# The first microseconds of a two-layer hybrid block: input in eight pieces in turn with weights, four dummy matmuls, and a yield between two groups of 32-row transposes

## The chip, the cores and the metric

The kernel runs on one core of a Trainium2 chip. The metric is the device time of one execution in microseconds (us); 2110.56 us is the median of three runs of the kernel before (2109.86 to 2110.83). Engines are named as in the profile: PE is the matrix engine (PEld its weight loads), DVE the vector engine, ACT the scalar engine, POOL the general one, SP the engine that issues most DMAs. "Granted clock" is the share of its full clock that PE was given, as the profile records it.

## The reference

The input x is 256 tokens by 2048. Layer 0 normalizes x, projects it, runs an S5 state-space mixer on one half and a gated recurrence (HGRN2) on the other, projects back and adds; then comes an MLP. Layer 1 does the same with sliding-window attention. Cut to what matters here:

```python
def rms_norm(x, gain):
    y = x * lax.rsqrt(jnp.mean(x * x, axis=-1, keepdims=True) + EPS)
    return y * gain

def reference(x, ...):
    h = x
    for layer in range(2):
        if layer == 0:
            y = s5_hgrn2_layer(rms_norm(h, even_norm[0]), even_w_in[0], ...)  # first product: xn @ w_in
        else:
            y = attention_layer(rms_norm(h, odd_norm[0]), ...)
        h = h + y
        h = h + squared_relu_mlp(rms_norm(h, mlp_norm[layer]), mlp_w_up[layer], mlp_w_down[layer])
    return h

# inside s5_mixer: B is scaled by a factor that is computed at run time
bbr = zr[..., None] * br - zi[..., None] * bi
bbi = zr[..., None] * bi + zi[..., None] * br
```

## The kernel before, in words

**Products.** Every weight matrix is cut into units of 512 KB, 704 in all, listed in the order of use in `units`. A unit is fetched into a tile `raw` (`emit_dma`, L86, four buffers), rounded to the 32-bit matmul type by ACT (`whi`, L93), and DVE subtracts to get the rest (`wlo`, L94). The activations are split in the same way into `XT.hi` and `XT.lo`. A product is three matmuls into one PSUM accumulator `acc`: whi times hi, whi times lo, wlo times hi (`mm`, L124, called by `wblock`, `ublock` and `xblock`). `advance` fetches up to six units ahead and splits up to three ahead, as far as buffers allow. In the first two blocks one unit holds two slices k of 128 rows and serves 24 matmuls of 256 columns.

**Start.** SP fetches x in four pieces of 512 columns (`load_x`, L244), with four weight units between them. ACT fetches the constants `cf` (with the identity) and the gain `even_norm`. PE runs eight dummy matmuls on a zeroed tile (`WARM`, L253), then turns the gain into columns (`vturn`, L270). Then `make_xT` transposes x: four transposes of 128 by 128 (L293) fill one PSUM tile with two slices k, ACT scales and rounds each into `XT0.hi` (L296), DVE makes `XT0.lo` (L297). With all four pieces listed ahead, the block loop begins: `wblock(XT0, K16)` for the first 512 columns of `even_w_in`.

**Side work.** Small work is written as generators in the list `side`. After each unit `pump(SIDE)` lets the first generator go on until it has yielded 1.5 us by its own estimates. `norm0` computes the row norms, `s5_prep` prepares the S5 matrices: in it 32 transposes (L436) turn the two halves of `Bn`, 16 each, from 32 partitions by 128 into 128 by 32. `s5_main` and `hgrn` follow. Their results are needed at fixed points, where `drain` runs them out. After the ten column blocks of `even_w_in`, the S5 result is split into `yg` (ACT L783, DVE L784), and the gate product `w_glu` starts.

**Order.** The code order is not the final one: a scheduler with a timeline model of its own merges the streams and decides each engine's order, so that a small edit moves instructions far behind it. What counts is each engine's final list, shown below for the places that matter.

Of the kernel before, what the change touches and what calls it, by code (L numbers as in the profile page):

```python
# [8 lines left out]
F32 = mybir.dt.float32  # L9
# [5 lines left out]
ALU = mybir.AluOpType  # L15
AX = mybir.AxisListType

P = 128
# [6 lines left out]
SIDE = 1.5  # L25
LOOK = 3
WARM = 8
LOOK_DMA = 6

NCF = 128 + 256 + 32 + 2  # L30
# [26 lines left out]
def hybrid_kernel(ctx: ExitStack, tc: tile.TileContext, x, even_norm, even_w_in, s5_lambda_re, s5_lambda_im,  # L57
                  s5_log_dt, s5_b_re, s5_b_im, s5_c_re, s5_c_im, s5_d, s5_w_glu, s5_b_glu, hgrn_lower_bound,
                  hgrn_o_norm, even_w_out, odd_norm, odd_w_qkv, q_norm, k_norm, att_sinks, odd_w_out,
                  mlp_norm, mlp_w_up, mlp_w_down, cfd, cmd, out, stop=None):  # L60
    nc = tc.nc
    V, S, G, PE = nc.vector, nc.scalar, nc.gpsimd, nc.tensor
# [10 lines left out]
    units = []  # L73
# [6 lines left out]
    raws, splits = {}, {}  # L80
    ptr = {"dma": 0, "split": 0, "use": 0}

    def emit_dma(i):
        W, kt, n0, nk = units[i]
        raw = wp.tile([P, nk, 1024 // nk], F32, tag="raw", name="raw", bufs=4)
        nc.sync.dma_start(out=raw, in_=W[kt * P:(kt + nk) * P, n0:n0 + 1024 // nk].rearrange("(k p) n -> p k n", p=P))  # L86
        raws[i] = raw

    def emit_split(i):
        raw, nk = raws.pop(i), units[i][3]  # L90
        hi = wp.tile([P, nk, 1024 // nk], F32R, tag="whi", name="whi")
        lo = wp.tile([P, nk, 1024 // nk], F32R, tag="wlo", name="wlo")
        S.copy(out=hi, in_=raw)  # L93
        V.tensor_tensor(out=lo, in0=raw, in1=hi.bitcast(F32), op=ALU.subtract)  # L94
        splits[i] = (hi, lo)

    def advance():
        i = ptr["use"]
        while ptr["dma"] < min(len(units), i + LOOK_DMA + 1) or ptr["split"] < min(len(units), i + LOOK + 1):
            if ptr["dma"] < min(len(units), i + LOOK_DMA + 1) and ptr["dma"] < ptr["split"] + 4:  # L100
                emit_dma(ptr["dma"])
                ptr["dma"] += 1
            else:
                emit_split(ptr["split"])
                ptr["split"] += 1
        ptr["use"] += 1
        return splits.pop(i)
# [67 lines left out]
    def pm(shape, dtype=F32):  # L175
        return psM.tile(shape, dtype, tag="m", name="m")

    def t4(shape, dtype=F32):
        return sp.tile(shape, dtype, tag="t4", name="t4")
# [60 lines left out]
    xt = cp.tile([P, 2, D], F32, tag="h", name="xt", bufs=1)  # L240
    xv = x[0].rearrange("(t p) n -> p t n", p=P)

    def load_x(q):
        nc.sync.dma_start(out=xt[:, :, q * 512:(q + 1) * 512], in_=xv[:, :, q * 512:(q + 1) * 512])  # L244

    cf = cp.tile([P, 130], F32, name="cf")
    load_x(0)
# [1 line left out]
    warm = t4([P, 512], BF16)  # L249
    V.memset(warm, 0.0)  # L250
    wps = pm([P, 512])
    for _ in range(WARM):
        PE.matmul(wps, warm[:, 0:P], warm, start=True, stop=True, skip_group_check=True)  # L253
    ident = cf[:, 0:128]
# [18 lines left out]
    def vc(name, i=0):  # L273
        k, c = vcol[name]
        return vec[k][:, c + i:c + i + 1]
# [1 line left out]
    vrow(0, "g0", even_norm.rearrange("o (k p) -> (o k) p", p=P), 16)  # L277
    cmt = cp.tile([P, 8, P], U8, tag="cm", name="cmt", bufs=1)

    for q, n in ((1, 1), (2, 2), (3, 0)):  # L280
        for _ in range(n):
            emit_dma(ptr["dma"])
            ptr["dma"] += 1
        load_x(q)
    vturn(0)

    def make_xT(src, XT, gain, kt0, nk):

        for a in range(kt0, kt0 + nk, 2):
            ps = pm([P, 2, T])  # L290
            for b in range(2):
                for t in range(2):
                    PE.transpose(ps[:, b, t * P:(t + 1) * P], src[:, t, (a + b) * P:(a + b + 1) * P], ident)  # L293
            for b in range(2):
                g = vc(gain, a + b)
                ihi = S.activation(out=XT.hi[:, a + b, :], in_=ps[:, b, :], func=AF.Copy, scale=g)  # L296
                ilo = V.scalar_tensor_tensor(out=XT.lo[:, a + b, :], in0=ps[:, b, :], scalar=g,  # L297
                                             in1=XT.hi[:, a + b, :].bitcast(F32), op0=ALU.mult, op1=ALU.subtract)
        return ihi, ilo

    XT0 = new_pair("x")
    for q in range(4):
        lastx = make_xT(xt, XT0, "g0", 4 * q, 4)


    rsx = cp.tile([P, 2], F32, name="rsx")
# [35 lines left out]
    def s5_prep():  # L342

        W = P
# [88 lines left out]
        for ri in range(2):  # L433
            bb = pm([P, 16, 32])
            for c in range(16):
                PE.transpose(bb[:, c, :], Bn[:, ri, :].rearrange("m (x c) -> m x c", c=16)[:, :, c],  # L436
                             ident[0:32, 0:32])
            bps.append(bb)

        def bc(v):  # L440
            return v.unsqueeze(1).to_broadcast([P, 16, 32])
# [19 lines left out]
        for ri in range(2):  # L461
# [3 lines left out]
            for h in range(2):  # L465
                ps = pm([P, 4, P])
                for f in range(4):
                    PE.transpose(ps[:, f, :], Cm[:, h * 4 + f].rearrange("p g w -> p (g w)"), ident)  # L468
                S.activation(out=CX[:, 0, ri, h * 16:h * 16 + 16, :].rearrange("p m c -> p (m c)"),
                             in_=ps.rearrange("p f w -> p (f w)"), func=AF.Copy, scale=-1.0 if ri else 1.0)  # L470
# [16 lines left out]
        for ri in range(2):  # L487
# [5 lines left out]
            for a in range(0, 16, 4):  # L493
                ps = pm([P, 4, P])
# [250 lines left out]
    for i in range(10):  # L745
# [3 lines left out]
        if i < 2:  # L749
            drain(n00)  # L750
            while "UY" not in st:
                pump(0.1)
            V.tensor_tensor(out=st["UY"][:, 4 * i:4 * i + 4, :], in0=acc,
                            in1=rsb.unsqueeze(1).to_broadcast([P, 4, T]), op=ALU.mult)
# [10 lines left out]
        for a in range(2):  # L765
            if j < 2:
                d2 = dst[:, a].rearrange("p (m t) -> p m t", m=2)
                V.tensor_tensor(out=d2, in0=acc[:, 2 * a:2 * a + 2, :],
                                in1=rsb.unsqueeze(1).to_broadcast([P, 2, T]), op=ALU.mult)
# [18 lines left out]
    for n in range(2):  # L788
# [4 lines left out]
        for a in range(2):  # L793
# [4 lines left out]
                            op=ALU.subtract)  # L798
# [86 lines left out]
    n0 = residual(yT, out0_passes, (lambda: Norm("g1")) if stop != "mix0" else Out, hwait)  # L885
# [145 lines left out]
    for t in range(2):  # L1031
        ps = pm([P, 4, P])
        for g in range(4):
# [4 lines left out]
                               in1=ka[0:64, :, ts_].bitcast(F32), op0=ALU.mult, op1=ALU.subtract)  # L1038
# [45 lines left out]
```

## Time and profile before

| what | value |
|---|---|
| three runs, median | 2110.56 us (2109.86 to 2110.83) |
| the profiled execution's own time | 2110.3 us |
| its span, first to last instruction | 2108.4 us |
| outside the span | 1.9 us |
| PE busy | 2096.6 us (99%) |
| DVE busy, ACT busy | 1333.9 us (63%), 1031.2 us (49%) |
| HBM read | 375.18 MB |

The profile is of one execution. Matmuls are pipelined, so that one lasts longer than the distance to the next; what a matmul costs is that distance. A line with a releaser ("<-") tells what ended an engine's idle time. The chain of waits is followed back from the last instruction. A window row gives for a stretch of time the busy time of an engine, the number of its instructions, the granted clock, the DMA engines' busy share and their rate.

### The profile page before, as it was taken

The page shows a single profiled execution, that of the slowest core. Times are in us where ns is not written, and L with a number is a line of the kernel's source. Part 1 is how long each engine was busy: PE and PEld are TensorE (multiplying, and loading weights), DVE is VectorE, ACT ScalarE, POOL GpSimd, SP SyncE. Part 2 cuts the span into 40 slices and gives each one's busy share as a digit, 9 for nine tenths or more (in the row PEclk, how much of TensorE's full clock was granted, in tenths as well). Part 3 has the DMA queues.
Part 4 walks back from the last instruction along what each step waited for, and adds up shares of the span by engine and source line. Part 5 has one row for each costly group of instructions (what it writes and reads, how often), then busy time and mean ns, then how long its engine had stood idle before and what let it go on. Part 6 is the DMA issues. An engine that isn't in the chain of part 4 may idle for free.

```text
span 2108.4 us, 29603 instructions
## 1 busy us (share of the span) xinstructions
PE 2096.6 (99%) x11628; PEld 1790.4 (85%) x11628; DVE 1333.9 (63%) x1859; ACT 1031.2 (49%) x1379; POOL 36.2 (2%) x36
## 2 busy tenths in 40 slices
PE   9999999999999999999999999999999999999999
PEld 8988888888888888888888888788888888888887
DVE  6799968765655565555555588765665565555544
ACT  5876554454443444344345477564443444344332
POOL 1000000000000000000000110000000000000000
PEclk8999999999999999999999999999999999999999
DMA  7455554566656666666656644456656666665664
GB/s 243 131 151 159 182 160 150 161 182 189 184 188 193 190 186 192 195 183 189 196 189 183 190 150 130 140 172 189 186 185 195 192 183 192 196 185 187 197 201 149
DMA packets 262859, 379.20 MB, mean 180 GB/s; under 512 B 14040, under 2 KB 145536, under 8 KB 262400
## 3 DMA queue, kind: packets, MB, share of 16 engines
q1 hardware_dynamic: 261296, 374.04, 57.6%
q0 software_dynamic: 672, 2.15, 0.3%
q8 instruction: 91, 1.49, 0.3%
q10 hardware_dynamic: 752, 1.12, 0.1%
q14 instruction: 48, 0.39, 0.1%
HBM read 375.18 MB, written 2.10 MB: 179 GB/s over the span
## 4 chain that ended last, share of the span: by engine, by line
PE 99%; DVE 0%; DMA 0%; ACT 0%; issue 0%; SPq 0%; DVEq 0%; ACTq 0%
PE acc L124 93%; PE m L124 4%; PE m L293 1%; PE m L977 1%; DMA xt<-in_x_dram 0%; PE m L436 0%; PE m L1011 0%; ACT whi L93 0%; PE m L496 0%; PE m L468 0%; DVE t L637 0%; PE m L718 0%; DVE t L613 0%; DVE clo L613 0%; DVE wlo L94 0%; DVE h L836 0%
## 5 line engine op out<-in xcount | busy, mean ns | idle before, releaser
L94 DVE TENSOR_TENSOR wlo<-raw,whi 128x1024 fp32r<-128x1024 f32 x704 | 861.9, 1225 | 687.2 <-ACT whi L93 686.7
L93 ACT CAST whi<-raw 128x1024 fp32r<-128x1024 f32 x704 | 738.7, 1050 | 973.7 <-PE acc L124 848.0
L124 PE MATMUL acc<-x,whi 128*128 128x512 f32 (+1 forms) x2944 | 893.9, 365 | 1.0 <-ACT x L783 1.0
L124 PE MATMUL acc<-x,wlo 128*128 128x256 f32 x2496 | 705.1, 283 | 0.0
L124 PEld LDWEIGHTS acc<-x,whi 128*128 128x128 f32 x2944 | 528.4, 190 | 97.6 <-ACT x L783 1.1
L124 PE MATMUL acc<-whi,chi 128*128 128x512 f32 x1280 | 500.1, 391 | 0.2 <-DVE h L836 0.2
L124 PE MATMUL acc<-whi,clo 128*128 128x512 f32 x1280 | 499.0, 390 | 0.0
L124 PE MATMUL acc<-wlo,chi 128*128 128x512 f32 x1280 | 498.9, 390 | 0.0
L124 PEld LDWEIGHTS acc<-x,wlo 128*128 128x128 f32 x2496 | 474.7, 190 | 1.5 <-issue 0.6
L124 PEld LDWEIGHTS acc<-whi,chi 128*128 128x128 f32 x1280 | 240.4, 188 | 50.5 <-issue 1.2
L124 PEld LDWEIGHTS acc<-whi,clo 128*128 128x128 f32 x1280 | 240.4, 188 | 49.5
L124 PEld LDWEIGHTS acc<-wlo,chi 128*128 128x128 f32 x1280 | 240.4, 188 | 48.9
L124 PE MATMUL acc<-whi,x 128*128 128x512 f32 x576 | 181.6, 393 | 0.0
L124 PEld LDWEIGHTS acc<-whi,x 128*128 128x128 f32 x576 | 107.5, 188 | 22.3 <-issue 1.0
L124 PE MATMUL acc<-wlo,x 128*128 128x512 f32 x288 | 113.3, 393 | 0.0
L124 PEld LDWEIGHTS acc<-wlo,x 128*128 128x128 f32 x288 | 54.1, 188 | 10.7
L866 DVE SCALAR_TENSOR_TENSOR h<-acc,rs2g,h 128x512 f32<-128x512 f32 x64 | 45.1, 747 | 21.3 <-PE acc L124 21.3
L852 DVE SCALAR_TENSOR_TENSOR t<-t 128x512 f32<-128x512 f32 x64 | 44.3, 692 | 2.2
L855 DVE TENSOR_TENSOR clo<-t,chi 128x512 fp32r<-128x512 f32 x64 | 43.8, 685 | 0.0
L851 DVE TENSOR_TENSOR t<-acc,t 128x512 f32<-128x512 f32 x64 | 43.8, 684 | 0.0
L854 ACT CAST chi<-t 128x512 fp32r<-128x512 f32 x64 | 39.3, 614 | 0.0
L850 ACT COPY t<-acc 128x512 f32<-128x512 f32 x64 | 37.0, 578 | 0.0
(204 smaller groups left out, 936.3 us busy)
## 6 DMA issues: line engine op xcount, KB each, us to landing
raw<-in_mlp_w_up_dram SPq DMA_DIRECT2D x256, 512.0 KB, 3.7
raw<-in_mlp_w_down_dram SPq DMA_DIRECT2D x256, 512.0 KB, 3.7
raw<-in_even_w_in_dram SPq DMA_DIRECT2D x80, 512.0 KB, 4.1
raw<-in_odd_w_qkv_dram SPq DMA_DIRECT2D x40, 512.0 KB, 3.6
raw<-in_even_w_out_dram SPq DMA_DIRECT2D x32, 512.0 KB, 3.7
raw<-in_odd_w_out_dram SPq DMA_DIRECT2D x32, 512.0 KB, 3.8
raw<-in_s_w_glu_dram SPq DMA_DIRECT2D x8, 512.0 KB, 3.8
xt<-in_x_dram SPq DMA_DIRECT2D x4, 512.0 KB, 8.4
```

The lines of the kernel that those rows point to most:

```text
L93: S.copy(out=hi, in_=raw)
L94: V.tensor_tensor(out=lo, in0=raw, in1=hi.bitcast(F32), op=ALU.subtract)
L124: PE.matmul(o, a, b, start=start, stop=stop, skip_group_check=True, **kw)
L293: PE.transpose(ps[:, b, t * P:(t + 1) * P], src[:, t, (a + b) * P:(a + b + 1) * P], ident)
L850: S.copy(out=r, in_=acc[:, :, 1])
L851: V.tensor_tensor(out=r, in0=acc[:, :, 0], in1=r, op=ALU.add)
L852: V.scalar_tensor_tensor(out=r, in0=r, scalar=0.0, in1=r, op0=ALU.max, op1=ALU.mult)
L854: S.copy(out=ch[c].hi[:, ks, :], in_=r)
L855: V.tensor_tensor(out=ch[c].lo[:, ks, :], in0=r, in1=ch[c].hi[:, ks, :].bitcast(F32), op=ALU.subtract)
L866: V.scalar_tensor_tensor(out=h[:, t, cs], in0=acc[:, t], scalar=norm.rs2[:, t:t + 1], in1=h[:, t, cs], op0=ALU.mult, op1=ALU.add)
L977: PE.transpose(ps[:, r, a, :], pr[:, 2 * a + r, k * P:(k + 1) * P], ident)
```

## The change

Five things are done. x is fetched in eight pieces of 256 columns (256 KB) instead of four of 512, with one weight unit between two pieces; pieces 5 to 7 are listed behind the fetch of weight units 4 to 6. The first weight unit is fetched and split in two halves, one for each slice k. `make_xT` is called for two slices at a time, with the split of a weight unit behind each of the first four calls. Four dummy matmuls (`REWARM`) are tied behind the last transpose of the first piece. In `s5_prep` a yield of 1.5 stands behind each group of 16 transposes.

```diff
+REWARM = 4
+    def pieces(i):
+        nk = units[i][3]
+        return [slice(k, k + 1) for k in range(nk)] if i == 0 else [slice(0, nk)]
...
-        nc.sync.dma_start(out=raw, in_=W[kt * P:(kt + nk) * P, n0:n0 + 1024 // nk].rearrange("(k p) n -> p k n", p=P))
+        src = W[kt * P:(kt + nk) * P, n0:n0 + 1024 // nk].rearrange("(k p) n -> p k n", p=P)
+        for ks in pieces(i):
+            nc.sync.dma_start(out=raw[:, ks], in_=src[:, ks])
...
-        S.copy(out=hi, in_=raw)
-        V.tensor_tensor(out=lo, in0=raw, in1=hi.bitcast(F32), op=ALU.subtract)
+        for ks in pieces(i):
+            S.copy(out=hi[:, ks], in_=raw[:, ks])
+            V.tensor_tensor(out=lo[:, ks], in0=raw[:, ks], in1=hi[:, ks].bitcast(F32), op=ALU.subtract)
...
-    for q, n in ((1, 1), (2, 2), (3, 0)):
-        for _ in range(n):
-            emit_dma(ptr["dma"])
-            ptr["dma"] += 1
+    for q in range(1, 5):
+        emit_dma(ptr["dma"])
+        ptr["dma"] += 1
         load_x(q)
...
-    for q in range(4):
-        lastx = make_xT(xt, XT0, "g0", 4 * q, 4)
+    for q in range(8):
+        lastx = make_xT(xt, XT0, "g0", 2 * q, 2)
+        if q == 0:
+            with tc.issue_after(lastx[2].ins):
+                for _ in range(REWARM):
+                    PE.matmul(wps, warm[:, 0:P], warm, start=True, stop=True, skip_group_check=True)
+        if q < 4:
+            emit_split(ptr["split"])
+            ptr["split"] += 1
+            if q < 3:
+                emit_dma(ptr["dma"])
+                ptr["dma"] += 1
+                load_x(5 + q)
...
             bps.append(bb)
+            yield 1.5
```

Lines of the changed kernel have other numbers: L253, L270, L293, L124, L420 and L436 of before are L262, L279, L301, L133, L439 and L455 there; the four new dummy matmuls are L315. L86 and L244, the fetches of weights and of x, are L94 and L253 there.

SP, the start of its list: `xt` is the tile of x, `raw` a weight unit (a half of it where the shape is 128x512). Before, and then changed:

```order
L244 DMA xt<-in_x_dram 128x2x512
L86 DMA raw<-in_even_w_in_dram 128x2x512
L244 DMA xt<-in_x_dram 128x2x512
L86 DMA raw<-in_even_w_in_dram 128x2x512 x2
L244 DMA xt<-in_x_dram 128x2x512 x2
L86 DMA raw<-in_even_w_in_dram 128x2x512
```

```order
L253 DMA xt<-in_x_dram 128x2x256
L94 DMA raw<-in_even_w_in_dram 128x512 x2
L253 DMA xt<-in_x_dram 128x2x256
L94 DMA raw<-in_even_w_in_dram 128x2x512
L253 DMA xt<-in_x_dram 128x2x256
...
L94 DMA raw<-in_even_w_in_dram 128x2x512
L253 DMA xt<-in_x_dram 128x2x256 x3
```

The first weight unit now stands behind 256 KB instead of 512, the second piece of x behind 768 KB instead of 1024, and the last three pieces behind the fifth weight unit.

PE, its start: `t_77` is the zeroed dummy tile, `t_90` the gain, `xt` the input, `acc` the first product. Before, and then changed:

```order
L253 MATMUL m<-t_77 128x512
L270 MATMUL m<-cf,t_90 128x16
L293 MATMUL m<-cf,xt 128x128 x16
L124 MATMUL acc<-x,whi 128x256 x2
L124 MATMUL acc<-x,wlo 128x256
```

```order
L279 MATMUL m<-cf,t_90 128x16
L301 MATMUL m<-cf,xt 128x128 x4
L315 LDWEIGHTS t_77
L315 MATMUL m<-t_77 128x512
...
L301 MATMUL m<-cf,xt 128x128 x4
L133 MATMUL acc<-x,whi 128x256 x2
L133 MATMUL acc<-x,wlo 128x256
```

Eight transposes instead of sixteen stand before the first matmul of the product, with four dummies (one shown) in their middle; the other transposes stand further down, four at a time.

PE, the 32-row transposes of `s5_prep` (`clo` holds `Bn`, `big` the S5 parameters). Before, and then changed:

```order
L124 MATMUL acc<-x,whi 128x256
L420 MATMUL m<-cf,big 128x32 x3
L436 MATMUL m<-cf,clo 128x32 x32
L124 MATMUL acc<-x,whi 128x256
L124 MATMUL acc<-x,wlo 128x256
```

```order
L133 MATMUL acc<-x,whi 128x256 x2
L439 MATMUL m<-cf,big 128x32 x3
L455 MATMUL m<-cf,clo 128x32 x32
L133 MATMUL acc<-x,wlo 128x256
L133 MATMUL acc<-x,whi 128x256 x2
```

All 32 still stand in one row. What moved is their place: 290 matmuls of `acc` stand ahead of them where 256 did.

PE, the end of the column blocks and the first matmuls of `w_glu` (`acc<-x,whi`); `m<-clo,t` are score matmuls of `hgrn`. Before, and then changed:

```order
L124 MATMUL acc<-whi,x 128x512
L124 MATMUL m<-clo,t_2424 32x32 x16
L124 MATMUL acc<-x,whi 128x256
L124 MATMUL m<-clo,t_2424 64x64 x8
L124 MATMUL acc<-x,whi 128x256
```

```order
L133 MATMUL acc<-whi,x 128x512
L133 MATMUL m<-clo,t_2435 128x128 x8
L133 MATMUL acc<-x,whi 128x256
L133 MATMUL m<-clo,t_2435 32x32 x16
L133 MATMUL acc<-x,whi 128x256
```

A group of eight score matmuls that stood among the last block's matmuls now stands behind them, and the 32x32 group has moved behind the first matmul of `w_glu`.

More of the change, by code (lines that the diff above doesn't have):

```diff
@@ L243, in load_x @@
     def load_x(q):
-        nc.sync.dma_start(out=xt[:, :, q * 512:(q + 1) * 512], in_=xv[:, :, q * 512:(q + 1) * 512])
+        nc.sync.dma_start(out=xt[:, :, q * 256:(q + 1) * 256], in_=xv[:, :, q * 256:(q + 1) * 256])
     cf = cp.tile([P, 130], F32, name="cf")
@@ L292, in make_xT @@
                 for t in range(2):
-                    PE.transpose(ps[:, b, t * P:(t + 1) * P], src[:, t, (a + b) * P:(a + b + 1) * P], ident)
+                    ipe = PE.transpose(ps[:, b, t * P:(t + 1) * P], src[:, t, (a + b) * P:(a + b + 1) * P], ident)
             for b in range(2):
@@ L298, in make_xT @@
                                              in1=XT.hi[:, a + b, :].bitcast(F32), op0=ALU.mult, op1=ALU.subtract)
-        return ihi, ilo
+        return ihi, ilo, ipe
     XT0 = new_pair("x")
-    for q in range(4):
-        lastx = make_xT(xt, XT0, "g0", 4 * q, 4)
+    for q in range(8):
[11 more added lines that the diff above has]
+                load_x(5 + q)
     rsx = cp.tile([P, 2], F32, name="rsx")
```

## The prediction

> **What bounds the kernel now.** I read the page first: its chain of work that ended last, by engine.
>
> ```profile
> PE 99%; DVE 0%; DMA 0%; ACT 0%; issue 0%; SPq 0%; DVEq 0%; ACTq 0%
> ```
>
> The time is PE's time. The change adds four dummy matmuls and removes no work, so it can gain only where PE waits or runs at less than its full clock. The three longest waits of PE, but for that on the launch (us in total, times, longest):
>
> ```profile
> PE m L270 <- DMA t<-in_even_norm_dram: 1.8, 1, 1.8
> PE m L293 <- DMA xt<-in_x_dram: 1.6, 1, 1.6
> ...
> PE acc L124 <- ACT x L783: 1.0, 1, 1.0
> ```
>
> Two of the three lie in the first 10 us. The clock shows more. Here are stretches of 3.41 us, cut where the granted clock changes (us, PE busy and number, granted clock, DMA share, GB/s):
>
> ```profile
> 0.49:3.91 3.42, 2.72 (x7) 1.00 0.42 122
> 3.91:7.32 3.41, 1.60 (x12) 1.00 1.02 303
> 7.32:10.73 3.41, 1.83 (x11) 0.50 1.05 392
> 10.73:14.15 3.42, 3.42 (x18) 0.50 1.06 385
> 44.87:48.28 3.41, 3.41 (x33) 1.00 0.08 10
> 48.28:51.69 3.41, 3.41 (x21) 0.50 0.83 253
> 51.69:55.11 3.42, 3.42 (x17) 0.50 0.30 66
> 55.11:58.52 3.41, 3.41 (x28) 1.00 0.38 138
> 85.82:89.23 3.41, 2.75 (x79) 1.00 0.45 131
> ```
>
> The clock is halved from 7.32 to 14.15 and from 48.28 to 55.11, and every change lies on one grid of 3.41 us. It fell behind a stretch that PE spent mostly idle (1.60 of 3.41), and behind one filled with the 32-row transposes. It came back behind stretches full of matmuls; not behind 48.28 to 51.69, which held the end of the transposes. The chain of the first 60 us, in order of time (start, us, what), gives the prices:
>
> ```profile
> 1.73 7.16 DMA xt<-in_x_dram
> 9.02 1.94 PE m L293 x8
> ...
> 16.84 0.87 PE m L293 x8
> ...
> 27.52 9.15 PE acc L124 x76
> ...
> 45.39 0.30 PE m L420 x3
> 45.69 3.55 PE m L436 x32
> 49.24 5.63 PE acc L124 x25
> ```
>
> A transpose takes 0.109 us at full clock (0.87 / 8) and 0.24 at half (1.94 / 8), a product matmul 0.120 (9.15 / 76) and 0.225 (5.63 / 25). Later slices of the page show the clock at nine tenths or more to the end:
>
> ```profile
> PEclk8999999999999999999999999999999999999999
> ```
>
> So these two places, and the wait on L783 near 296 us, are where something can be won or lost.
>
> **The start, part by part.** PE's timeline there, then ACT's and DVE's:
>
> ```profile
> 1.19 3.22 PE L253 MATMUL m<-t 128*128 128x512 bf16 x8 [1.19 <-DVE chi L519]
> 6.22 0.20 PE L270 MATMUL m<-cf,t 16*128 16x16 f32 x1 [1.81 <-DMA t<-in_even_norm_dram]
> 6.35 1.09 PE L293 MATMUL m<-cf,xt 128*128 128x128 f32 x8
> ...
> 10.61 0.78 PE L124 MATMUL acc<-x,whi 128*128 128x256 f32 x2
> ```
>
> ```profile
> 6.82 1.04 ACT L93 CAST whi<-raw 128x1024 fp32r<-128x1024 f32 x1 [3.81 <-DMA raw<-in_even_w_in_dram]
> 7.77 0.17 ACT L271 COPY vec<-m 128x16 f32<-128x16 f32 x1
> 7.97 0.84 ACT L296 ACTIVATE x<-m,vec 128x256 fp32r<-128x256 f32 x2
> ```
>
> ```profile
> 9.04 0.87 DVE L297 SCALAR_TENSOR_TENSOR x<-m,vec,x 128x256 fp32r<-128x256 f32 x2
> ```
>
> *Fetches.* By the windows 0.42 MB are in by 3.91 us (3.42 x 122) and 1.45 MB by 7.32. The first weight unit, 1.11 MB with the constants, would be through at 6.2, and ACT took it at 6.82; the second piece of x (1.64 MB) at 7.8, and PE took it at 9.02. So landing lies 0.6 to 1.2 us behind. Changed, the first unit is complete behind 0.85 MB: 5.35 plus that, some 6.2. The second piece of x, behind 1.11 MB, lands at 6.8 to 7.4, the third (1.9 MB) at 9.1 to 9.7. Rows of half the length cost little: the page's part on DMA issues shows weight units with rows of 1 KB (w_up) landing as fast as those of 2 KB (w_down).
>
> ```profile
> raw<-in_mlp_w_up_dram SPq DMA_DIRECT2D x256, 512.0 KB, 3.7
> raw<-in_mlp_w_down_dram SPq DMA_DIRECT2D x256, 512.0 KB, 3.7
> ```
>
> On SP's queue pieces 5 to 7 stand behind the fifth unit, which waits for DVE's split of the first unit (about 7.5 us); they are needed only after 20 us, at 2.9 us of PE for each unit (24 x 0.120). I cost that at nothing; its cover is that distance.
>
> *Splitting.* ACT: first unit's second half at 6.2, about 0.55 (half of 1.04), gain columns 0.17, hi of one slice 0.42 (0.84 / 2): 7.35. DVE's lo takes 0.44 (0.87 / 2): operands ready at 7.8, where before the last was ready past 10.6.
>
> *PE.* The gain's landing stays, at 6.22; it is not in SP's queue. Four transposes (0.44) from 6.35 to 6.8. Four dummies: before, eight took 3.22 us, a distance of some 0.43 at half clock, so 0.215 at full. Two fit before 7.32, the others end near 8.05. The stretch 3.91 to 7.32 still has PE idle from 4.4 to 6.2, more than half, so I expect the clock to fall at 7.32 as before. The second piece's four transposes at 0.22 to 0.24 end at 8.9, and the product starts there: 1.65 us earlier than at 10.54. The dummies thus cost up to 1.1 us of the earlier start; what they buy is a busy stretch.
>
> From 7.32 on PE has no gap, so the clock should come back at 10.73 instead of 14.15. Work done by 14.15 in full-clock time: before, 16 transposes (1.74) and 3.6 us at half (1.8), 3.55. Changed, 8 transposes (0.87), 1.83 us at half (0.92), 3.42 at full: 5.2. **Gain 1.65 us.** The unknown is whether the stretch counts as busy: transposes and dummies fill half of it. Nearest rows: the groups of the stretch 85.82 to 89.23.
>
> ```profile
> L496 PE MATMUL m<-cf,big 128*128 128x128 f32 x11 | 1.4, 272 | 0.0
> L124 PE MATMUL acc<-x,whi 128*128 128x256 f32 x4 | 0.8, 280 | 0.0
> L124 PE MATMUL m<-CX,big 128*32 128x32 f32 x62 | 0.7, 199 | 0.0
> L124 PE MATMUL acc<-x,wlo 128*128 128x256 f32 x2 | 0.7, 334 | 0.0
> ```
>
> Six product matmuls (0.72 us) and eleven full transposes (1.2 us) kept the clock at 1.00 there, so full transposes do seem to count. If they don't, the gain is 0 (second rival).
>
> **The 32-row transposes.** The yield doesn't separate them: PE's list still has 32 in a row, 3.55 us long. The edit itself is worth nothing. But their place on the grid moves: 34 more product matmuls ahead (4.1 us) less the gain of 1.65 put L420 at 47.8 instead of 45.39, the transposes from 48.1 to 51.65. Then they fill 48.28 to 51.69, the clock falls at 51.69, the next stretch holds matmuls alone, and it returns at 55.11: 3.41 us at half, a loss of 1.7. Before, 5.87 of the 6.83 us at half were matmuls (from 49.24 on): 2.9. **Gain 1.2**, for any start of the transposes from 46.8 to 48.9; otherwise some 0.4. That holds if the grid lies as in this execution, which one profile cannot show.
>
> **Order further on.** At the start of `w_glu` eight score matmuls come late, and with them the chain that the 32x32 group waits for:
>
> ```profile
> 293.68 1.34 DVE t L637 x2
> 295.03 0.57 DVE t L613
> 295.59 0.61 DVE clo L613
> ```
>
> These 2.5 us ran beside product matmuls; now they start behind the last of them, together with the wait on L783 that is there anyway (from 295.56 to the second `w_glu` matmul at 299.0). I put the extra wait at 0.3 us, between 0 and 0.9. Other places up to 440 us are reordered too, with no side to prefer: 0, plus or minus 0.5.
>
> **Sum.** On the profiled execution's 2110.3 us (span 2108.4 and 1.9 around it): -1.65 - 1.2 + 0.3 = -2.55, so 2107.75. The median, 2110.56, is 0.26 above that execution: **2108.0 us**. A difference of 0.2% is 4.2 us and is about what a measurement of this kernel can tell from no change; this forecast lies within it.
>
> The page "TensorE: Matmul & The Clock Gate" of the Trainium skill (Part 1) describes half clock as the resting state, left after a busy window of about 3.4 us on a free-running grid; the trace agrees, with its steps at 7.32, 14.15, 48.28 and 55.11. Free-running would mean that another execution has the grid elsewhere, and that no single count of the second gain is safe; the three runs lie within 0.97 us.
>
> **Rivals.**
>
> *The clock never falls (15%).* If the gain lands half a us earlier, or the dummies make the stretch to 7.32 busy enough, full clock holds. The dummies end at 7.65, the second transposes at 8.1; by 14.15: 0.87 + 6.05 = 6.9, a gain of 3.35. The 32-row transposes then start at 46.4 and gain 0.4: 2110.56 - 3.35 - 0.4 + 0.3 = 2107.1. Against it: that stretch was 1.60 of 3.41 busy and fell.
>
> *Transposes don't count as busy (22%).* Then 7.32 to 10.73 holds only some 0.7 us of dummies and 1.8 of matmuls, 2.5 of 3.41 or 74%, the share of 48.28 to 51.69 (49.24 to 51.69: 2.45 us), which did not bring the clock back. Half clock to 14.15: 0.87 + 5.25 / 2 = 3.5, gain 0. The transposes start at 49.8, gain 0.4; sum -0.1: 2110.5. For it: that row. Against it: the stretch at 85.82. The same page (Part 4) says that transpose-mode work doesn't count as PE-busy in the same way; by that rule the sum would be this rival's.
>
> *The second drop goes as well (8%).* Should the 32 transposes straddle a grid line, neither stretch may be empty enough: 1.7 us more, 2106.3, and 2104.6 from the rival above.
>
> *A new drop, slower (10%).* The stretch at 85.82 stood at 2.75 of 3.41 busy; one at 1.60 fell. The same groups (16, 12 and 4 transposes with thin matmuls) move by 2 to 4 us on the grid. If a stretch there falls to about half busy, the clock halves for 3.41 to 6.83 us: 1.7 to 3.4 us. That decides from the point where it exceeds the start's gain: 2110.5 + 1.7 to 3.4, or 2112 to 2114.
>
> **How the numbers follow.** Forecast 45% (2107 to 2109), rivals 15, 22, 8 and 10. Range 2105.5 to 2111.0: it takes in the forecast, the first two rivals and half of the third, with plus or minus 0.5 for the reordering. Faster by over 0.2% (below 2106.3) needs the third rival or a lucky first one: 0.14. Slower by over 0.2% (above 2114.8) needs two new drops: 0.03. The rest, 0.83, is within.
>
> **What would show it.** Right: first product matmul at 8 to 9 us, granted clock 1.00 from 10.73 or one grid step before 14.15; 32 transposes in a row with half clock for one step behind them; the first product block ending about 1.6 us earlier for the same count. Wrong: clock at 0.50 to 14.15, a wait of PE on `xt` or `whi` between 9 and 25 us (fetches too late), or a new stretch at 0.50 beyond 60 us.

## The result and the profile after

The changed kernel is slower: 2122.3 us, median of four runs (2122.04 to 2126.65), against 2110.2 for the kernel before on the same chip. The ratio is 1.0062, with a 95% interval of 1.0049 to 1.0076. That is 12.1 us, beyond the 0.2% bound and outside the range. The profiled execution took 2122.2 us, its span 2120.3; 11.9 of the 12.1 us are therefore in the trace. Line numbers below are those of the changed kernel unless "before" is said.

The chain that ended last, by engine, was 99% PE. Now something else ends it for a part of the time:

```profile
PE 95%; DVE 2%; ACT 1%; issue 1%; DMA 1%; POOL 0%; DVEq 0%; SPq 0%; ACTq 0%
```

PE's waits in the changed kernel (us in total, times, longest):

```profile
PE m L738 <- DVE t L734: 5.0, 1, 5.0
PE m L133 <- DVE t L574: 2.0, 1, 2.0
PE m L133 <- DVE clo L633: 1.6, 1, 1.6
PE acc L133 <- ACT chi L741: 1.6, 2, 0.8
...
PE m L516 <- ACT clo L517: 1.0, 1, 1.0
PE m L301 <- DMA xt<-in_x_dram: 0.9, 2, 0.7
PE m L279 <- DMA t<-in_even_norm_dram: 0.5, 1, 0.5
```

The two waits of the start, 1.8 and 1.6 us before, are down to 0.5 and 0.9: the change did what it says there. Of the first four lines three are new and the third, L633, stood at 0.6 us before (as L613); none of them is at the start. L574 is a step of S5 (`s5_main`), L633 one of HGRN (`hgrn`), L734 to L741 the last steps of an HGRN half. The start itself, PE's timeline:

```profile
5.30 0.20 PE L279 MATMUL m<-cf,t 16*128 16x16 f32 x1 [0.53 <-DMA t<-in_even_norm_dram]
5.44 0.66 PE L301 MATMUL m<-cf,xt 128*128 128x128 f32 x4
5.93 1.03 PE L315 MATMUL m<-t 128*128 128x512 bf16 x4
7.63 0.65 PE L301 MATMUL m<-cf,xt 128*128 128x128 f32 x4 [0.67 <-DMA xt<-in_x_dram]
8.04 0.48 PE L133 MATMUL acc<-x,whi 128*128 128x256 f32 x2
```

The product begins at 8.04 instead of 10.61. The granted clock, in stretches of its grid in this execution (us, PE, PEld, DVE, ACT and POOL busy with their numbers, granted clock, DMA share, GB/s):

```profile
4.84:8.25 3.41, 2.27 (x15) 1.53 (x16) 2.07 (x4) 2.25 (x5) 1.64 (x5) 1.00 1.00 259
45.80:49.22 3.42, 3.42 (x33) 3.29 (x32) 2.72 (x5) 2.35 (x3) 0.00 (x0) 1.00 0.39 141
49.22:52.63 3.41, 3.41 (x23) 3.35 (x23) 1.68 (x6) 0.00 (x0) 0.00 (x0) 0.50 0.76 214
...
178.92:182.34 3.42, 3.42 (x11) 2.70 (x10) 3.42 (x9) 2.92 (x5) 0.00 (x0) 0.50 0.46 142
301.80:305.22 3.42, 3.42 (x16) 3.42 (x17) 3.42 (x6) 1.44 (x8) 0.00 (x0) 0.50 0.00 0
414.44:421.27 6.83, 4.50 (x20) 4.13 (x20) 1.14 (x4) 1.29 (x3) 1.01 (x1) 0.50 0.22 77
```

The fall at the start is gone; the one behind the 32-row transposes stayed, two steps long, to 56.04; three new ones came (at 178.92, 301.80 and 414.44), one at each of the first three waits of the list. The record of the clock begins at 4.84; the eight dummies ahead of it still ran some 0.43 us apart, the half-clock distance.

**Where the 12 us came from.** The 10144 product matmuls (those into `acc`) stand in the same order in both kernels but for 35 that change places with near neighbours, so the start of the n-th can be compared. Read from the two traces:

| product matmul no. | place | before, us | changed, us | difference |
|---|---|---|---|---|
| 0 | first | 10.61 | 8.04 | -2.6 |
| 400 | before S5's long part | 71.60 | 68.91 | -2.7 |
| 1000 | middle of S5 | 188.69 | 192.63 | +3.9 |
| 1520 | ahead of `w_glu` | 290.36 | 291.74 | +1.4 |
| 2000 | residual product | 404.46 | 405.44 | +1.0 |
| 2040 | in its third pass | 414.45 | 429.12 | +14.7 |
| 3000 | in the first MLP | 591.01 | 603.09 | +12.1 |
| 10143 | last | 2103.46 | 2115.11 | +11.6 |

The gain of the start is real and holds to no. 400 and beyond; no. 800 still starts 4.6 us ahead of before. It is lost in S5, between no. 800 and 1000. Its steps stand up to 55 product matmuls later than before at first and are back at the places of before by no. 937, where PE waits 2.0 us for L574. The largest step is the 13.7 us between no. 2000 and 2040, in the last steps of HGRN's second half.

Not all of the 13.7 us is lost. Up to no. 1000 PE has run the same small matmuls in both kernels but for the four new dummies; at no. 2000 the changed kernel is 36 behind (32 of HGRN's `m<-qf` and four transposes), at no. 2040 level again. At 0.112 us each (1.79 / 16, below) these 36 are 4.0 us of work that has only moved. So some 9.7 us are lost at the tail, and the -3.0 us between no. 1000 and 2000 is really a loss of 1.0.

The chain at the tail, in order of time, changed (start, us, what):

```profile
409.00 1.80 PE m L133 x16
...
411.31 1.06 ACT whi L102
...
412.39 1.23 DVE wlo L103
413.61 0.61 DVE hss L729
...
414.49 1.02 POOL hrs L731
...
415.53 0.36 DVE t L734
...
416.03 0.45 PE m L738
416.48 3.42 PE m L133 x16
419.89 0.65 PE m L738 x3
...
420.57 0.70 ACT chi L741
```

And before, where L734 and L738 are L714 and L718:

```profile
401.24 0.44 PE m L718 x4
401.68 1.79 PE m L124 x16
403.46 2.10 PE acc L124 x9
...
407.89 1.05 DVE t L714 x4
```

Before, the chain over ACT, DVE and POOL ran beside product matmuls. In the changed kernel PE stands through it, from 411.0 to 416.0, the clock halves meanwhile, and 16 small matmuls that took 1.79 us take 3.42. PE's list says why (each `m<-qf` of the list shows as two in the trace). `L718` (changed `L738`) are the last transposes of HGRN, four for each half of the tokens; between the two groups of four before:

```
1568 L718 MATMUL m<-cf,t_3428 128x128 x4
     (eight matmuls m<-qf, then 27 product matmuls)
1604 L718 MATMUL m<-cf,t_3428 128x128 x4
```

and in the changed kernel:

```
1596 L133 MATMUL m<-qf,t_3433 128x128 x4
1597 L133 MATMUL m<-qf,t_3435 128x128 x4
1598 L133 MATMUL acc<-whi,clo 128x512
1599 L738 MATMUL m<-cf,t_3439 128x128
     (eight matmuls m<-qf)
1608 L738 MATMUL m<-cf,t_3439 128x128 x3
     (12 product matmuls)
1620 L738 MATMUL m<-cf,t_3439 128x128 x4
```

One product matmul is left between the matmuls that start the chain and the transpose that needs its end. The residual's third pass begins with product matmul no. 2016 and reads what comes of the first group, from no. 2028 on also what comes of the second. Counted in this way the two groups stand behind 1995 and 2022 before, 21 and 6 product matmuls ahead of their readers, and behind 2016 and 2028 in the changed kernel: nothing is left to run beside them. In the trace of before, PE first reads `yT.lo` of the second group at 412.64 (`whi,clo`), 0.7 us behind its end:

```profile
411.19 0.75 DVE L722 SCALAR_TENSOR_TENSOR clo<-m,vec,chi 128x512 fp32r<-128x512 f32 x1
```

That was all the slack of this chain's last result.

My theory ("order"): the edits at the start made the scheduler draw up another order for the side work, and the loss is the price of that order. Rivals: the added yields, the dummies, the late pieces of x by themselves, and an early start that the side work cannot follow.

### The profile page after: what moved, and what is told of

It is laid out like the page before. It is cut to its first block, busy times and chain, and to the rows that moved or that the text cites. A ratio compares the mean times of both kernels' runs of the same rounds, so it can differ in the third digit from the quotient of the medians.

```text
span 2120.3 us, 29622 instructions
## 1 busy us (share of the span) xinstructions
PE 2101.0 (99%) x11632; PEld 1792.4 (85%) x11632; DVE 1333.1 (63%) x1860; ACT 1032.8 (49%) x1380; POOL 36.4 (2%) x36
## 4 chain that ended last, share of the span: by engine, by line
PE 95%; DVE 2%; ACT 1%; issue 1%; DMA 1%; POOL 0%; DVEq 0%; SPq 0%; ACTq 0%
PE acc L133 89%; PE m L133 4%; DVE t L574 1%; PE m L301 1%; PE m L997 1%; DVE wlo L103 0%; DMA xt<-in_x_dram 0%; DVE t L589 0%; ACT whi L102 0%; ACT big L512 0%; ACT t L551 0%; PE m L455 0%; PE m L1031 0%; ACT t L550 0%; DMA cf<-in_consts_dram 0%
## 5 line engine op out<-in xcount | busy, mean ns | idle before, releaser
L103 DVE TENSOR_TENSOR wlo<-raw,whi 128x1024 fp32r<-128x1024 f32 (+1 forms) x705 | 860.3, 1221 | 689.3 <-ACT whi L102 688.8
L102 ACT CAST whi<-raw 128x1024 fp32r<-128x1024 f32 (+1 forms) x705 | 739.6, 1050 | 979.4 <-PE acc L133 848.8
L133 PE MATMUL acc<-x,whi 128*128 128x512 f32 (+1 forms) x2944 | 891.3, 365 | 0.1
L133 PE MATMUL acc<-x,wlo 128*128 128x256 f32 x2496 | 702.6, 282 | 0.0
L133 PEld LDWEIGHTS acc<-x,whi 128*128 128x128 f32 x2944 | 527.9, 190 | 95.8 <-issue 0.4
L133 PE MATMUL acc<-whi,chi 128*128 128x512 f32 x1280 | 500.1, 391 | 1.6 <-ACT chi L741 1.6
L133 PE MATMUL acc<-whi,clo 128*128 128x512 f32 x1280 | 498.8, 390 | 0.0
L133 PE MATMUL acc<-wlo,chi 128*128 128x512 f32 x1280 | 498.7, 390 | 0.0
L133 PEld LDWEIGHTS acc<-x,wlo 128*128 128x128 f32 x2496 | 473.8, 190 | 1.2 <-issue 0.6
L133 PEld LDWEIGHTS acc<-whi,chi 128*128 128x128 f32 x1280 | 240.4, 188 | 52.4 <-ACT chi L741 2.1
L133 PEld LDWEIGHTS acc<-whi,clo 128*128 128x128 f32 x1280 | 240.4, 188 | 49.3
L133 PEld LDWEIGHTS acc<-wlo,chi 128*128 128x128 f32 x1280 | 240.4, 188 | 49.1
L133 PE MATMUL acc<-whi,x 128*128 128x512 f32 x576 | 182.4, 394 | 0.0
L133 PEld LDWEIGHTS acc<-whi,x 128*128 128x128 f32 x576 | 108.3, 189 | 22.9 <-issue 0.8
L133 PE MATMUL acc<-wlo,x 128*128 128x512 f32 x288 | 114.3, 397 | 0.2 <-DVE wlo L103 0.2
L133 PEld LDWEIGHTS acc<-wlo,x 128*128 128x128 f32 x288 | 54.5, 189 | 11.6 <-DVE wlo L103 0.6
```

Of the source, the lines that this page charges most:

```text
L102: S.copy(out=hi[:, ks], in_=raw[:, ks])
L103: V.tensor_tensor(out=lo[:, ks], in0=raw[:, ks], in1=hi[:, ks].bitcast(F32), op=ALU.subtract)
L133: PE.matmul(o, a, b, start=start, stop=stop, skip_group_check=True, **kw)
```

## The experiments

Ratios are to the kernel before on the same chip, with 95% intervals; medians of before were 2108.7 to 2109.6 us, against the 2110.2 beside the changed kernel. A difference in us to the changed kernel is therefore good to about 1 us; the ratios are the safer comparison.

**One part undone or alone.** First unit whole again:

```diff
-        return [slice(k, k + 1) for k in range(nk)] if i == 0 else [slice(0, nk)]
+        return [slice(k, k + 1) for k in range(nk)] if False else [slice(0, nk)]
```

> The changed kernel with one part undone: the first weight unit is loaded and split whole, as before the change. All else of the change stays (x in eight pieces in turn with the units, early splits, dummies, the added yields). In TensorE's written order this puts the HGRN steps back at the places they had before the change (second half's last transposes behind product matmuls 1995 and 2022; in the changed kernel behind 2016 and 2028), while the 32-row transposes stand at 269 (before 256, changed 290). Theory 'order' (the loss of 12 us comes from the new places of the HGRN steps, so that residual pass 2 waits for them): 2107 to 2110 us, no wait of 5 us at the line of the HGRN transposes, no half-clock stretch near 414 us. Rival 'yields' (the two added yields push the S5 and HGRN work two units later): 2119 to 2123, since the yields stay. Rival 'pieces of x and interleaved queue' (the late x pieces delay norm0 and with it all side work): 2119 to 2123.

2116.9 us, ratio 1.0038 (1.0023 to 1.0053): between the two forecasts. The tail behaved as "order" said: no wait at the HGRN transposes, no half clock near 414 us, and from no. 1400 on the difference to before is constant, +4.5 us. But a loss of 5.5 us stayed between no. 400 and 1400, where S5 steps now stand up to 40 product matmuls earlier than before and PE waits for them:

```profile
PE m L516 <- ACT clo L517: 2.1, 1, 2.1
PE m L133 <- DVE t L574: 1.8, 4, 0.9
```

Two losses, then, and "order" has to explain both. The yields taken out:

```diff
             bps.append(bb)
-            yield 1.5
```

> The changed kernel without the added yield of 1.5 behind each group of 32-row transposes; TensorE's written order is that of the changed kernel. Theory 'order': 2121 to 2123 us. Rival 'yields': 2107 to 2111.

2121.8 us, 1.0059 (1.0044 to 1.0074): the yields do nothing. The dummies taken out:

```diff
-        if q == 0:
-            with tc.issue_after(lastx[2].ins):
-                for _ in range(REWARM):
-                    PE.matmul(wps, warm[:, 0:P], warm, start=True, stop=True, skip_group_check=True)
```

> The changed kernel without the four dummy matmuls behind the first transposes; the HGRN steps stand nearly as in the changed kernel (last transposes behind 2016 and 2028). Theory 'order': the loss stays, 2121 to 2125 us; if the dummies are what held the clock at the start, a half-clock stretch near 8 us comes back and adds 1 to 2 us. Rival 'dummies' (the dummies stand ahead of the product and their cost or their shift of the order makes the loss): 2108 to 2112.

2119.6 us, 1.0049 (1.0034 to 1.0064), 1.4 us under the forecast of "order". The loss stays, if 2.7 us smaller, with the wait at the HGRN transposes (3.9 us), so the dummies are not the cause. The clock did not fall at the start in the profiled execution, though PE was busy for 1.93 of 3.41 us there:

```profile
6.12:9.53 3.41, 1.93 (x16) 1.93 (x17) 2.00 (x5) 1.93 (x6) 1.46 (x3) 1.00 1.00 354
```

But here the grid lay 1.3 us later than in the profile of the changed kernel (6.12 against 4.84), and twelve of the 16 matmuls in the stretch belong to the product. Whether the clock would hold without dummies on the grid of that profile is not shown.

Before, with only the first unit in two pieces (diff as in the change, `pieces`):

> The kernel before with one part of the change alone: the first weight unit in two pieces. Written order of TensorE as before the change. Theory 'order': 2108.5 to 2110.5 us, since the same edit that sets off the new order in the changed kernel does not set it off here. A rival by which splitting the first unit costs time itself: 2112 or more.

2110.0 us, 1.0004 (0.9994 to 1.0013). The product starts at 8.07 here too, but the clock fell behind a stretch with 1.52 us busy, and all of the gain was gone by no. 80. The edit that brings on the new HGRN places in the changed kernel does not do so here. Before, with only the eight pieces in turn with the units:

> The kernel before with one part of the change alone: x in eight pieces, in turn with the weight units (units whole, no early splits, no dummies, no added yields). Written order of TensorE at S5 and HGRN as in the run with the first unit whole (S5 steps up to 30 product matmuls earlier than before, HGRN as before). Theory 'order': the S5 loss of that run, without its gain at the start: 2112 to 2118 us, no wait at the HGRN transposes. Rival (the turn costs nothing by itself, the loss needs the dummies or the early splits): 2108 to 2111.

2116.7 us, 1.0035 (1.0021 to 1.0048): the S5 loss of e1, 5.5 us between no. 400 and 1400, with the same waits (2.1 and 1.8 us), from this one part.

**The order put back.** Only the turn of the first transfers as before, all else as changed, but for one early split of four that goes with it:

```diff
-    for q in range(1, 5):
-        emit_dma(ptr["dma"])
-        ptr["dma"] += 1
-        load_x(q)
+    load_x(1)
+    for q, n in ((1, 1), (2, 2), (3, 0)):
+        for _ in range(n):
+            emit_dma(ptr["dma"])
+            ptr["dma"] += 1
+        load_x(2 * q)
+        load_x(2 * q + 1)
...
-        if q < 4:
+        if q < 3:
             emit_split(ptr["split"])
             ptr["split"] += 1
-            if q < 3:
-                emit_dma(ptr["dma"])
-                ptr["dma"] += 1
-                load_x(5 + q)
```

> The changed kernel with only the order of the first transfers put back to that of before (x in eight pieces, but in the old turn: the first half of x ahead of the second and third unit, all of x ahead of the fourth); two pieces of the first unit, early splits, dummies and added yields stay. TensorE's written order is then that of before to within 12 matmuls at every S5 step and exactly that of before at the HGRN steps. Theory 'order' (the 12 us come from the new places of the S5 and HGRN steps, not from the early start): 2105.5 to 2108.5 us, the product starts near 8 us and no wait at S5 or HGRN steps is longer than before. Rival 'early start' (the side chain has only about 2.5 us of slack, so that every gain at the start comes back as waits at S5 or HGRN steps): 2109 to 2115.

2109.6 us, 1.0001 (0.9992 to 1.001). The whole loss is gone, with pieces, dummies, three of the splits and yields still in. But the gain is not there either: the mechanism is that of "order", the time lies in the range of the rival "early start". In its trace the product is 2.6 us ahead to no. 1000 and 1.5 from 1400 on; what went in between is a wait for DVE at an S5 step (L573 here), which before did not have:

```profile
PE m L133 <- DVE t L573: 1.7, 2, 1.2
```

Eight dummies instead of four in the changed kernel:

```diff
-REWARM = 4
+REWARM = 8
```

> The changed kernel with eight dummies behind the first transposes instead of four: more work at the start, about 1 us. In the written order it puts the HGRN steps back ahead of the residual (last transposes behind product matmuls 1995 and 2022 instead of 2016 and 2028), and the S5 steps up to 30 product matmuls ahead of those of before. Theory 'order': 2112 to 2119 us, no wait of 5 us at the HGRN transposes and no half clock near 414 us, with waits left at the S5 steps as in the run with the first unit whole. Rival 'late side work' (the dummies and the late pieces of x delay the side chain, whatever the written order): 2122 to 2125.

2111.5 us, 1.0009 (1.0000 to 1.0018): more work at the start, and 10.8 us less than the changed kernel. The last HGRN transposes stand behind 1995 and 2022 again, and these waits at S5 and `w_glu` are the longest left:

```profile
PE m L516 <- ACT clo L517: 1.6, 1, 1.6
PE acc L133 <- ACT x L803: 1.5, 1, 1.5
```

It beat its forecast by half a us; the S5 steps, up to 66 product matmuls earlier than before, cost 4.2 us between no. 400 and 1400 where e1 lost 5.5. How far the S5 steps move does not tell the price.

**The HGRN tail, with the start left alone.** HGRN's gate and k on ACT instead of DVE, in the changed kernel. The start and the order up to the middle of S5 stay as changed:

```diff
-            V.tensor_scalar(out=fg[:, h], in0=fg[:, h], scalar1=lbt[:, 3, c:c + 1], scalar2=lbt[:, 2, c:c + 1],
-                            op0=ALU.mult, op1=ALU.add)
+            S.activation(out=fg[:, h], in_=fg[:, h], func=AF.Identity, scale=lbt[:, 3, c:c + 1],
+                         bias=lbt[:, 2, c:c + 1])
...
-        V.tensor_scalar(out=k, in0=fg, scalar1=-1.0, scalar2=1.0, op0=ALU.mult, op1=ALU.add)
+        S.activation(out=k, in_=fg, func=AF.Identity, scale=-1.0, bias=1.0)
```

> The changed kernel with HGRN's gate (four scale-and-add steps of 0.43 us) and k = 1 - gate (0.70 us) computed on ScalarE instead of VectorE, for both halves, 4.8 us in all. TensorE's written order stays that of the changed kernel up to the middle of S5 (32-row transposes behind 290, block transposes behind 463 and 532), later S5 steps stand up to 35 product matmuls later, and the last HGRN transposes stand behind 1995 and 2022, as in before, instead of 2016 and 2028. Theory 'order at the HGRN tail': no wait of 5 us there, no half clock near 414 us, 2107 to 2113 us, with a wait of about 2 us left at an S5 step. Rival 'the S5 steps or the late x make the loss and the HGRN tail only shows it': 2118 to 2123.

2109.6 us, 1.0002 (0.9993 to 1.0011): 12.7 us less than the changed kernel, by an edit of 4.8 us of DVE work. Its chain at the tail reads like that of before:

```profile
400.65 0.44 PE m L738 x4
401.09 1.79 PE m L133 x16
402.88 2.10 PE acc L133 x9
...
407.31 1.05 DVE t L734 x4
```

No. 2000 starts 0.6 us ahead of before and no. 2040 0.5 us ahead: the tail's loss is gone. The edit did more than that, though. Later S5 steps stand up to 39 product matmuls behind their places in the changed kernel, the wait of 2.0 us there is down to 0.5 (the forecast left 2), and no. 1000 starts at 186.82 where it started at 192.63. So nearly half of the gain lies ahead of the tail.

For the tail itself all profiles agree. The last transposes stand behind 2016 and 2028 in three of them (changed, e2, e3), and each has a wait of 3.9 to 5.0 us there with half clock around it; in the ten with 1995 and 2022 (before, e1, e4 to e8, e13 to e15) none has. That the places of these steps make the tail's loss is shown, with the start left as the change has it; and as e6 and this run still fetch x in turn, the late pieces are not the price by themselves. The control, the same edit in the kernel before:

> The control: before with the gate and k on ScalarE. Both theories: within 1 us of before (2108.5 to 2110.5), since before waits 1.3 us at S5 and HGRN steps together; if it gains as much as e14 does over e7, the gain has nothing to do with the change.

2113.1 us, 1.0019 (1.0010 to 1.0027), 4.2 us slower, against both forecasts: there the edit draws S5 steps up to 38 product matmuls forward, and PE waits for them (L554 is L574 of the changed kernel). The profiled execution, at 2110.9, is the fastest of eleven, so its trace shows the wait but not all of the 4.2 us:

```profile
PE m L124 <- DVE t L554: 2.8, 2, 2.1
```

So the edit is no gain in itself; what it does to the order is.

**The 32-row transposes really separated.** On e5, the first group written ahead of the S5 parameters' transposes:

```diff
+        turn_b(0)
         Cn = t4([P, 2, 8, 64])
...
-        for ri in range(2):
-            bb = pm([P, 16, 32])
-            (16 transposes)
-            bps.append(bb)
-            yield 1.5
+        turn_b(1)
+        yield 1.5
```

> The kernel of e5_x_order_back in which the first group of sixteen 32-row transposes is written ahead of the transposes of the S5 parameters, so that the groups really come apart in TensorE's order (behind product matmuls 187 and 251, where both stood behind 256). Theory that a stretch filled by 32-row transposes halves the clock: no half-clock stretch between 40 and 60 us, and 1.5 to 3.5 us less than e5_x_order_back: 2103 to 2106 us. Rival, by which 16 of them (1.8 us) are still enough or the stretch comes from something else: the time of e5_x_order_back within 0.7 us. A rival by which the S5 steps, 20 product matmuls later in the order, wait: 2 us or more over e5_x_order_back.

2108.8 us, 1.0000 (0.9991 to 1.0009), 0.8 us under e5: both forecasts missed, the rival's by 0.1. The chain shows the groups apart, and in this execution the clock stayed at 1.00 from 4.72 to 2103.92:

```profile
34.62 1.87 PE m L439 x16
...
44.37 0.30 PE m L448 x3
44.66 1.77 PE m L439 x16
```

In e9 and e12, further down, the groups lie in the same places, and there the clock did fall for one step, from 47.80 and from 46.66. In e9 the whole second group and three transposes of L448, 2.1 us, lay in one stretch of the grid:

```profile
44.39:47.80 3.41, 3.41 (x31) 3.37 (x31) 2.65 (x8) 0.00 (x0) 0.00 (x0) 1.00 0.58 154
47.80:51.22 3.42, 3.42 (x19) 3.42 (x18) 1.22 (x1) 1.04 (x1) 0.00 (x0) 0.50 0.49 158
```

In e7 a grid line at 45.7 cut that group in two, and in e14, below, one at 46.0. So where a grid line cuts the second group the fall is gone (e7, e14), and where none does one step is left (e9, e12); theory and rival each hold for a part of the grid.

At no. 400 the product was 4.8 us ahead of before, at no. 1000 1.6: the clock's gain was there and S5 took it. With the gate and k on ACT as well:

> e7_separated with the gate and k on ScalarE. Theory 'VectorE's pace in S5 swallows the gain': some 2 of the 4.8 us lie ahead of the last Gelu, so 1 to 2.5 us less than e7_separated: 2105.5 to 2108 us. Rival 'the order, not VectorE's load, fixes the waits': e7_separated within 0.8 us, or more if the new order has waits of its own.

2108.4 us, 0.9998 (0.9989 to 1.0007): the best version made, some 13 us under the changed kernel and not to be told from before. The theory on DVE's pace missed; the 0.4 us to e7 lie within what the rival, "order", allows.

**Splits on POOL.** Every third `wlo` between units 30 and 72 on POOL, in e7, in the changed kernel and in before, and every fourth in e7:

```diff
-            V.tensor_tensor(out=lo[:, ks], in0=raw[:, ks], in1=hi[:, ks].bitcast(F32), op=ALU.subtract)
+            (G if i % 3 == 0 and 30 <= i < 72 else V).tensor_tensor(out=lo[:, ks], in0=raw[:, ks], in1=hi[:, ks].bitcast(F32), op=ALU.subtract)
```

> The kernel of e7_separated in which the subtraction of every third weight split between units 30 and 72 (14 of 42) runs on GpSimd instead of VectorE. VectorE is busy 76.8 of the 80 us from 180 to 260 in that run, and 39 splits of 1.235 us are 47.9 us of the 130 us from 130 to 260 in the profile of before. Theory 'VectorE paces the side steps': 14 times 1.24, 17 us, leave VectorE, the last Gelu of S5 comes 5 to 15 us earlier, the waits at the S5 steps go, the gain of the start and of the clock near 50 us reaches the end: 2103 to 2107 us. Rival 'GpSimd is too slow or disturbs VectorE': the splits come late, TensorE waits for wlo, 2110 us or more. Rival 'no room': the side steps were not what held the gain, 2108 to 2110.

> The changed kernel with the same third of the splits on GpSimd and nothing else. In the written order the last HGRN transposes come behind product matmul 1988 instead of 2028. Theory 'order, paced by VectorE': the wait of 5 us at the HGRN transposes and the half clock near 414 us go, 2105 to 2112 us. Rival 'the late start of the side work itself costs the 12 us': 2118 or more.

> The control: the kernel before with the same third of the splits on GpSimd. The last HGRN transposes come behind product matmul 1916 instead of 2022. Theory: before has little to gain there (its waits at S5 and HGRN steps are 1.3 us together), 2106.5 to 2110 us. Rival 'GpSimd is too slow or disturbs VectorE': 2111 or more.

> As e9_sep_pool3 with every fourth split (10 of 42) on GpSimd: theory 'VectorE paces the side steps': within 1.5 us of e9_sep_pool3, 2103 to 2107.5; rival 'GpSimd is too slow': less of its loss, between e7_separated and e9_sep_pool3.

2126.8, 2127.2, 2126.0 and 2122.9 us (1.0081, 1.0085, 1.0078 and 1.0064): all far slower, before too. The theory's four forecasts missed, and the rivals' hold by their numbers. One split takes more than twice as long on POOL as on DVE (1.22 us in the changed kernel); the row of e9, with 14 of them:

```profile
L103 POOL TENSOR_TENSOR wlo<-raw,whi 128x1024 fp32r<-128x1024 f32 x14 | 40.4, 2887 | 169.4 <-ACT whi L102 152.7 <-DVE t L660 10.4 <-PE acc L133 6.1
```

and the order is drawn up for S5 steps 100 product matmuls and more earlier than without, which the chip does not deliver. PE's wait in e11, the control:

```profile
PE m L124 <- DVE t L554: 11.4, 8, 3.0
```

In e10 the HGRN tail was free of waits and the loss sat in S5, so its number speaks for the rival, "late start", but its trace does not. As a test of DVE's pace these four fail, since they moved the order more than DVE's load.

## Why the prediction was wrong

**The step that failed** is one clause: "Other places up to 440 us are reordered too, with no side to prefer: 0, plus or minus 0.5." The places were worth +6.6 us between no. 400 and 1000, some +1.0 from there to no. 2000, and some +9.7 at one place, the HGRN tail (with moved work taken out, as above). A new stretch at half clock beyond 60 us, which the prediction named as a sign that it is wrong, came three times. The side was to be had: before, the HGRN tail had 0.7 us to spare, and the lists of both kernels, counted in product matmuls, show its last transposes pushed back to their readers. The prediction spoke of PE's list at the start and at `w_glu` alone and gave the rest a symmetric allowance. e13 and e6 show that the places decide, e2 that the yields do not, and e5 that without the new turn of the transfers neither loss arises. The turn alone brings the loss in S5 (e8); the one at the tail needs the halved first unit as well (e1, e4). Why a place in S5 costs what it does was not found.

**The start** came out better than the forecast: the product at 8.04 against 8.9, the clock at 1.00 from 4.84 on. That is the first rival, held at 15%; where it put the gain at 3.35 us, no. 80 starts 2.4 and no. 200 2.9 us ahead. The gain columns landed 0.9 us sooner (5.30 against 6.22), so the stretch to 8.25 was 2.27 of 3.41 us busy. How much of that the dummies are worth stays open (e3).

**Transposes as busy time.** The stretch 4.84 to 8.25 held the clock with 2.27 us busy, most of them dummies and full-size transposes; stretches with 1.60 (before) and 1.52 (e4) fell. That alone does not tell what counts, but a stretch of e1 does. It held with 1.89 us busy, most of it twelve full-size transposes; without them 0.4 us is left, or 0.7 with what overlaps them:

```profile
85.95:89.36 3.41, 1.89 (x44) 1.00 0.06 22
```

```profile
L516 PE MATMUL m<-cf,big 128*128 128x128 f32 x12 | 1.5, 272 | 0.0
```

Two stretches of the changed kernel with more than that and no transposes at all fell:

```profile
175.51:178.92 3.41, 1.42 (x9) 1.00 0.75 188
298.39:301.80 3.41, 1.66 (x41) 1.00 0.43 148
```

So the rival "transposes don't count" is out for full-size ones. The Trainium skill, page "TensorE: Matmul & The Clock Gate", Part 4, says transpose mode doesn't count as PE-busy in the same way: for the 32-row ones the trace agrees, since the clock fell behind 45.80 to 49.22, busy for 3.42 of 3.42 us and from 47.0 us on filled with transposes from 32 partitions (L439, L455), and with 2.1 us of them in one stretch too (e9), while a stretch with less than that held (e7). For the full-size ones the row of e1 speaks against it. Whether the 32-row ones fail to count because they transpose or because they are small was not tried.

**The 32-row transposes.** "The edit itself is worth nothing" was right. The gain of 1.2 from their place on the grid did not come: half clock lasted 6.83 us again. The mechanism was right, the place was luck. In the 13 profiles with 32 in a row the fall lasted one step where their start lay between 1.6 us ahead of a grid line and 0.1 us behind it (e2, e3, e4, e6, e8, e13, e15), and two where it lay 0.7 to 1.4 us behind one (before, changed, e1, e5, e10, e11). The grid lies 0.49 us off a multiple of 3.413 in the profile of before and 1.43 off in that of the changed kernel, so one execution's grid could not carry that term. Part 1 of the same page of the Trainium skill calls the window free-running; the runs agree.

**At `w_glu`** I put 0.3 us, at most 0.9; the wait on L633 is 1.6 us and a half-clock stretch follows it (301.80), worth 1.7: together some 3 us.

**The slower rival** had the right sign and a wrong mechanism: new falls of the clock did come, three of them, but with waits that the new order made, not by a shift on the grid.

What stays open in part: why the start's gain of about 2.5 us does not reach the end even where the order is that of before (e5). A part of the answer is the yardstick. The profiled execution of before, 2110.3 us at a mean clock of 0.996, had both falls two steps long. On the chip of e5 only 8 of 27 executions of before show 0.996 (2110.2 to 2111.1 us); the other 19, at 0.998 or 0.999, take 2107.7 to 2109.8. Against the profile of before e5 ends 1.5 us ahead, against the median it gains nothing. The other 1.1 us go at an S5 step that waits for DVE, and before, DVE is busy for 77.4 of 80 us there:

```profile
180.00:260.00 80.00, 79.89 (x660) 72.70 (x659) 77.40 (x155) 50.94 (x60) 2.08 (x3) 1.00 0.55 162
```

That DVE's pace swallows them is likely, but only argued: e9 to e12 and e14 do not show it.

## What to carry to other kernels

Where a scheduler merges streams, a change is worth what the whole new order is worth. Compare the lists of every engine up to the last point where side work must be done, counted in the bounding engine's main instructions, and price each side step whose distance to its consumer shrank by the chain behind it. A gain at the start is only as good as the slack of the tightest side chain, here 0.7 us at one place.

## What the runs showed that was not expected

- **Idle time is paid twice.** A wait of 5.0 us in the tail cost some 9.7: half clock came with it (16 small matmuls 3.42 us instead of 1.79), and the steps from the transposes to the residual's matmuls, hidden before, stood open twice (no. 2016 starts at 421.31, no. 2028 at 426.26).
- **Small edits set off or cure 10 us.** Four more dummies (e6) or 4.8 us of DVE work moved to ACT (e13) took out 10.8 and 12.7 us.
- **Product matmuls of the first MLP ran faster in the changed kernel,** 2.6 us over nos. 2040 to 3000, as they did in e2, e3 and e11, and in none of the runs with HGRN's old places. The groups of `w_up` from 520 to 600 us, before and changed, with as many more matmuls in the same time:

```profile
L124 PE MATMUL acc<-x,whi 128*128 128x512 f32 x228 | 80.6, 399 | 0.0
```

```profile
L133 PE MATMUL acc<-x,whi 128*128 128x512 f32 x232 | 80.5, 394 | 0.0
```

  The cause was not tried.
